# Persistent tiles of a hybrid stream encoder, put in another order in SBUF

## The chip, the cores and the metric

The kernel runs on one core of a Trainium2 chip. The metric is the device time of one execution in microseconds (us), lower is better. Three runs of the kernel before took 1451.21, 1452.49 and 1453.37 us.

## The reference, cut to what matters

One layer over 256 tokens of 2048 channels in float32. The normalised input goes through one wide projection (22672 columns) that feeds four token mixers; their outputs are projected again, gated, summed, and projected once more.

```
h = rms_norm(x, norm_g)
u = einsum('bsd,dn->bsn', h, w_in)
a_in, b_in, b_gate, c_qkv, c_f, c_gate, d_in, d_gate, m_logit = split(u)
y_a = short_conv(a_in)              # A: gated short convolution
y_b = rwkv7(b_in, b_gate, ...)      # B: RWKV-7 time mixing, 16 heads of 64
y_c = fox(c_qkv, c_f, c_gate)       # C: forgetting attention, 16 heads of 64
y_d = pooling(d_in, d_gate)         # D: causal pooling
proj = einsum('bskc,kcd->bskd', stack(y_a..y_d), w_branch)      # 4 x 1024 -> 2048
merged = sum(sigmoid(m_logit + b_merge) * proj, over the branches)
out = rms_norm(x + einsum('bsd,de->bse', merged, w_out), final_g)
```

## The kernel before, in words

Nearly all the work is matrix products of 256 tokens with weights that come from DRAM. A product is made in three single-pass matmuls: each float32 operand is split in a high part (rounded to the type F32R) and a low part (the difference), and high x high, high x low and low x high are added up in PSUM (`products`, lines 236, 237 and 238). The moving operand is a row block of weights, 128 x 512 (`wh` or `wl`); the stationary operand is a 128 x 128 piece of the transposed activations (`xh`, `xl` for the input projection; `yah`, `yal` to `ydh`, `ydl` for the branches; `mh`, `ml` for the output).

`chunk` makes 512 output columns. For each pair of row blocks (KG = 2) one DMA on SP's queue brings the raw weights (`raw`, 3 buffers), ACT writes the high parts (`wh`, 6 buffers, line 263), DVE the low parts (`wl`, 6 buffers, line 264), and TensorE runs 2 blocks of tokens x 2 row blocks x 3 matmuls. A chunk of the input projection has 16 row blocks, so 96 matmuls; one of a branch's projection has 8, so 48. In the last chunk of the output projection (`keep`) the parts of the weights lie in tiles whose contents are no longer needed: `xh`, `xl`, `ych`, `ycl`, `ydh`, `ydl`.

The program runs through branches B, C, A (in halves of 512 channels) and D; their chunks of the input projection are mixed by the scheduler with RWKV's and attention's small steps. It sets a static order by priority: weights' conversion first, then RWKV's chain, then attention's, then the rest. Then comes the merge: 4 groups of 512 columns x 4 branches, each step one chunk for the gate (96 matmuls) and one for the branch (48). The output projection is 4 chunks, and a norm and the stores end it.

Tiles are laid out in each partition in the order of the pools, and within a pool in the order in which the tiles are first asked for; each size is rounded up to 32 bytes. The pool `pers` comes first: `cst` (constants, 5120 bytes a partition), `xh`, `xl` (16384 each), then seven small tiles (`rstd`, `nrstd8`, `ngT`, `ones1`, `cq`, `fss`, `frs`: the first four where the input is read, the others further down; 352 bytes in all with rounding). Then come `wpool` (`raw`, `wh`, `wl`), `bc`, `ynat` (`yb`, `yc`, `ya`, later `mh` and the first of `ml`), `wk`, and from line 757 on `ytp` (branches' transposed outputs and `ml1`). The first byte of `pers` lies at remainder 128 modulo 512.

Of the kernel before, what the change touches and what calls it, by code (L numbers as in the profile page):

```python
# [9 lines left out]
F32 = mybir.dt.float32  # L10
F32R = mybir.dt.float32r
# [6 lines left out]
P = 128  # L18
# [35 lines left out]
    ("cmask", 384),  # L54
# [10 lines left out]
def make_constants():  # L65
    """Constants of the shapes alone: masks, cumulative sums, pooling bands."""
    i = np.arange(P)[:, None]
    t = np.arange(P)[None, :]
    c = {}
    c["ident"] = (i == t)  # L70
    c["cmat"] = ((i <= t).astype(np.float32) - (i % SUB <= SUB // 2 - 1)) * (i // SUB == t // SUB)
    c["tri"] = (i <= t)
    c["ones"] = np.ones((P, P))
    c["rmask"] = np.concatenate([(i % SUB < t[:, :SUB]), (i % SUB <= t[:, :SUB])], axis=1)
    caus = np.where(i >= t, 0.0, -NEG)
    c["cmask"] = np.concatenate([caus, np.zeros((P, P)), caus], axis=1)
    slot = np.arange(P) % 32
    rep = slot // NH
    ii = np.arange(32)[None, :, None]
    cc = np.arange(8)[None, None, :]  # L80
    c["eye32"] = (ii == rep[:, None, None] * 8 + cc).reshape(P, 256)
    consts = np.concatenate([np.asarray(c[n], np.float32).reshape(P, w) for n, w in _CONST_COLS], axis=1)
    s = np.arange(T)[:, None]
    t = np.arange(T)[None, :]
    bands = []
    for win in POOL_WINDOWS:
        band = ((s <= t) & (s > t - win)).astype(np.float32) / np.minimum(t + 1, win) - (s == t)
        bands.append(band[:P])
        bands.append(band[P:, P:])
    bands = np.concatenate(bands, axis=1).astype(np.float32)  # L90
    return np.ascontiguousarray(consts), np.ascontiguousarray(bands)
# [3 lines left out]
def kernel(  # L95
# [38 lines left out]
    # ---------------------------------------------------------------- pools  # L134
# [11 lines left out]
    # Of what is ready, the scheduler takes the weights' conversion first, then the chains of  # L146
    # small steps of branches B and C, then the rest in the order of the program.
# [10 lines left out]
    # ------------------------------------------------------------ constants  # L158
# [5 lines left out]
    def K(name):  # L164
        lo, hi = _COFF[name]
        return cst[:, lo:hi]
# [3 lines left out]
    def bcast(src, n=CH, pool=bc_pool):  # L170
        """A row of DRAM on every partition."""
        t = pool.tile([P, n], F32, name="row", bufs=2)
        gp.dma_start(out=t, in_=src.unsqueeze(0).to_broadcast([P, n]))  # L173
        return t
# [7 lines left out]
    # ----------------------------------------------------- input, RMS, x^T  # L182
    xh = pers.tile([P, D // P, T], F32R, name="xh")
    xl = pers.tile([P, D // P, T], F32R, name="xl")
    rstd = pers.tile([P, NB], F32, name="rstd")
    nrstd8 = pers.tile([P, NB], F32, name="nrstd8")
    ngT = pers.tile([P, D // P], F32, name="ngT")
    ones1 = pers.tile([P, 1], F32, name="ones1")
# [8 lines left out]
    def x_quarter(q):  # L197
        """x^T * norm_g, split in two parts, of 512 channels; the sums of squares for the norm."""
        xt = xin.tile([P, NB, CH], F32, name=f"x{q}")
        nc.sync.dma_start(out=xt, in_=x_v[:, :, q * CH:(q + 1) * CH])  # L200
        if q == 0:
            tp = psum_ex("c")
            nc.tensor.transpose(tp[:, 0:16], ng16, ident[:16, :16])
            v.tensor_copy(out=ngT, in_=tp[:, 0:16])
        for k2 in range(2):
            tp = psum_ex("c" if k2 else "r")
            for j in range(2):
                for b in range(NB):
                    c0 = (2 * k2 + j) * P
                    nc.tensor.transpose(tp[:, j * T + b * P:j * T + (b + 1) * P], xt[:, b, c0:c0 + P], ident)  # L210
            for j in range(2):
                k = q * 4 + k2 * 2 + j
                s = tp[:, j * T:(j + 1) * T]
                sc.activation(out=xh[:, k, :], in_=s, func=AF.Copy, scale=ngT[:, k:k + 1])
                v.scalar_tensor_tensor(out=xl[:, k, :], in0=s, scalar=ngT[:, k:k + 1],
                                       in1=xh[:, k, :].bitcast(F32), op0=ALU.mult, op1=ALU.subtract)
        return xt
# [13 lines left out]
    # --------------------------------------------- products in three passes  # L231
# [11 lines left out]
    def chunk(ranges, nk, sth, stl, before=lambda g: None, keep=None):  # L243
        """[T, n] = st^T @ w for column ranges (view [P, nk, .] in DRAM, first, number) of the weights.
        With keep, where the parts of all the weights have place, the second tokens follow the first."""
# [36 lines left out]
    def silu_psum(dst, ps):  # L282
        """dst = silu(rstd * ps) on [P, NB, CH]."""
# [6 lines left out]
    def gate(dst, ps):  # L290
        """dst *= silu(rstd * ps) on [P, NB, CH]."""
# [7 lines left out]
    def shift(dst, src, n):  # L299
        """dst[t] = src[t - n], zero before the first token; [P, NB, cols]."""  # L300
# [5 lines left out]
    # ------------------------------ the first chunk, with the input beside it  # L306
# [21 lines left out]
    # ---------------------------------------------------- RWKV-7 (branch B)  # L328
# [11 lines left out]
    def hbc(t):  # L340
        """[P, n] -> [P, n, H]."""
        return t.unsqueeze(2).to_broadcast([P, t.shape[1], H])

    def rwkv_prep(hf, u):
        """Everything of a half (8 heads) that is made in [token, channel]: u and what is returned."""
# [9 lines left out]
        # decay and in-context learning rate  # L355
        s = rw.tile([P, NB, HALF], F32, name="s")
        a = rw.tile([P, NB, HALF], F32, name="a")
        # three products of parts, the two with the high part of the weights in one
# [18 lines left out]
        # the norm of the keys goes to one side: kk kk^T / |kk|^2  # L377
# [9 lines left out]
        # keys scaled by the in-context learning rate  # L387
# [5 lines left out]
        # bonus weights per head  # L393
# [6 lines left out]
        # decay from the middle of one sub-block to the middle of the next  # L400
# [11 lines left out]
        # decays relative to the middle of each sub-block  # L412
        ba = rw.tile([P, NB, HALF], F32, name="pv")
        for b in range(NB):
# [11 lines left out]
            # b and k of each sub-block on the two halves of the partitions  # L426
# [4 lines left out]
        # values of even sub-blocks on the upper partitions  # L431
# [4 lines left out]
    def rwkv_block(hf, b, u, prep):  # L436
        """128 tokens, two sub-blocks, of 8 heads."""
# [4 lines left out]
        # [a | r | b | k] with channels on partitions, a pair of heads at a time  # L442
# [15 lines left out]
        # products of tokens: G[b | k of s, head, sub-block, a | r of t], with s before t  # L458
# [12 lines left out]
        # inverse of the 32x32 diagonal blocks by substitution: a quadrant holds (sub-block, block),  # L471
        # a partition of it a head and 8 of the 32 columns
# [23 lines left out]
        # 32 -> 64: the block above the diagonal is U00 M01 U11  # L496
# [18 lines left out]
        # of each sub-block: what its keys' removals turn out to be (lower half), its values (upper half)  # L515
        uv1 = rw.tile([P, HALF], F32, name="e2")
        sc.activation(out=uv1[hi], in_=vv[hi], func=AF.Copy)
        for e in range(2):
# [3 lines left out]
            # z (lower half) and y (upper half) from the state, from the keys of the sub-block  # L522
# [34 lines left out]
        # norm over each head, bonus, gate  # L557
# [23 lines left out]
    # ------------------------------------- low-rank inputs and forget gates  # L581
    cq = pers.tile([P, NB, 16], F32, name="cq")
    loraT = rw.tile([P, 2, T], F32R, name="loraT")

    def lora_and_forget(lu, cf):
# [10 lines left out]
        # the high part of each on its half of the partitions, the low part on the other  # L596
# [5 lines left out]
        # cumulative log forget gates c[t, head]  # L602
        bfb = bcast(fox_bf[0], 16)
        v.tensor_tensor(out=cf, in0=cf, in1=mid(bfb), op=ALU.add)
        fa = wk.tile([P, NB, 16], F32, name="fa")
# [13 lines left out]
    # ------------------------------------------------------- FoX (branch C)  # L619
# [19 lines left out]
    def fox_head(hf, h, qa, ka, vt):  # L639
# [13 lines left out]
        for b, s in ((0, slice(0, P)), (1, slice(P, 3 * P))):  # L653
            # the logits are negated: their least is minus the maximum
            v.tensor_tensor_reduce(out=pt[:, s], in0=lg[:, s], in1=K("cmask")[:, s], scale=1.0, scalar=-2 * NEG,  # L655
# [19 lines left out]
    # ------------------------------------------------ short conv (branch A)  # L675
# [24 lines left out]
    # ------------------------------------------------------------- schedule  # L700
    def b_inputs(hf):
        t = [rw.tile([P, NB, HALF], F32, name="u" + nm) for nm in "rkv"]
        c0 = O_B + hf * HALF
        for j in range(3):
            if j == 2 and hf == 1:
                # the last columns of v with those of the low-rank inputs and the forget gates
# [49 lines left out]
    # -------------------------------------------- transposed branch outputs  # L756
# [3 lines left out]
    def split_T(dst, k0, src, nk):  # L760
        """dst (high, low parts)[:, k0 + k, token] from src [token, block, channel]."""
# [19 lines left out]
    # --------------------------------------------------- pooling (branch D)  # L781
# [30 lines left out]
    # ------------------------------------------------------- gated merge  # L812
# [15 lines left out]
    # ------------------------------------- output projection, final norm  # L828
# [12 lines left out]
    # the last weights' parts take the place of x^T and of two branches' outputs  # L841
# [9 lines left out]
    fss = pers.tile([P, NB, 4], F32, name="fss")  # L851
    frs = pers.tile([P, NB], F32, name="frs")
# [56 lines left out]
```

## Time and profile before

| | |
|---|---|
| median of 3 runs | 1452.49 us |
| profiled execution, span from first to last instruction | 1453.2 us |
| TensorE (PE) busy | 1424.5 us, 98% |
| weight loads (PEld) | 1147.8 us, 79% |
| VectorE (DVE) | 987.4 us, 68% |
| ScalarE (ACT) | 738.1 us, 51% |
| moved by DMA | 266.24 MB, mean 183 GB/s |

The profiled execution is known by its span alone, and the span stands within the three runs. A matmul's busy time runs to the modelled end of a pipelined instruction, so neighbours overlap; how fast matmuls follow each other is read from their start times in the timeline.

### The profile page before, as it was taken

The numbers are of one execution on the slowest core, as the hardware profiler recorded it, in microseconds if no ns is written. First come the engines' busy times: TensorE is split into PE (matmuls) and PEld (weight loads), VectorE is DVE, ScalarE is ACT, GpSimd is POOL, SyncE is SP. The second block draws the span as 40 slices with busy tenths as digits, with TensorE's granted clock in tenths as the row PEclk, the third lists the DMA queues.
The fourth block names the chain that finished last, engine by engine and source line by source line (L and its number), as shares of the span: only waits on it lengthen the run. The fifth ranks groups of instructions, "written<-read, shape, count | busy, mean of one in ns | idle before, by whom it ended". The sixth has DMA issues, their size and how long they took to land.

```text
span 1453.2 us, 19581 instructions
## 1 busy us (share of the span) xinstructions
PE 1424.5 (98%) x6913; PEld 1147.8 (79%) x6913; DVE 987.4 (68%) x1719; ACT 738.1 (51%) x1278; POOL 68.5 (5%) x135
## 2 busy tenths in 40 slices
PE   7999999999999999999999999999999999999997
PEld 5887778887877678887888888888888888888886
DVE  4558888599766889579957656565666556556654
ACT  6455645654455455554435544444445444444554
POOL 2110000001011000010000000000000000000000
PEclk9999999999999999999999999999999999999999
DMA  8776545446557645545544566666666666676664
GB/s 251 198 217 200 175 131 174 131 146 196 161 174 205 185 144 176 158 143 185 189 145 145 169 194 198 198 187 202 198 187 191 198 196 193 222 226 194 196 204 146
DMA packets 136626, 266.24 MB, mean 183 GB/s; under 512 B 11577, under 2 KB 15848, under 8 KB 136528
## 3 DMA queue, kind: packets, MB, share of 16 engines
q1 hardware_dynamic: 128768, 240.95, 52.4%
q0 software_dynamic: 7760, 24.04, 6.6%
q8 instruction: 54, 0.88, 0.3%
q14 instruction: 44, 0.36, 0.1%
HBM read 257.51 MB, written 2.10 MB: 179 GB/s over the span
## 4 chain that ended last, share of the span: by engine, by line
PE 81%; DVE 7%; DMA 6%; issue 3%; ACT 2%; POOL 0%; SPq 0%; ACTq 0%; DVEq 0%; POOLq 0%
PE psm L237 24%; PE psm L238 24%; PE psm L236 24%; DVE wl L264 3%; DMA raw<-in_w_in_dram 2%; DVE MT L478 1%; PE ps_r L464 1%; DMA pv<-ur 1%; DMA cg<-pz 1%; ACT wh L263 1%; PE ps_r L537 1%; DMA pv<-uv 1%; DVE tm L485 1%; PE ps_z L554 1%; PE ps_c L804 1%
## 5 line engine op out<-in xcount | busy, mean ns | idle before, releaser
L263 ACT ACTIVATE wh<-raw 128x512 fp32r<-128x512 f32 (+1 forms) x896 | 547.4, 624 | 553.7 <-PE psm L238 386.9
L264 DVE TENSOR_TENSOR wl<-raw,wh 128x512 fp32r<-128x512 f32 (+1 forms) x896 | 599.1, 681 | 327.0 <-ACT wh L263 323.5
L237 PE MATMUL psm<-wl,xh 128*128 128x512 f32 (+1 forms) x1440 | 570.5, 397 | 4.3 <-DVE wl L264 3.7
L238 PE MATMUL psm<-wh,xl 128*128 128x512 f32 (+1 forms) x1440 | 569.6, 397 | 0.0
L236 PE MATMUL psm<-wh,xh 128*128 128x512 f32 (+1 forms) x1440 | 552.6, 396 | 4.6 <-ACT wh L263 4.3
L237 PEld LDWEIGHTS psm<-wl,xh 128*128 128x128 f32 x1440 | 271.4, 189 | 71.6 <-DVE wl L264 10.5
L236 PEld LDWEIGHTS psm<-wh,xh 128*128 128x128 f32 x1440 | 271.0, 189 | 70.2 <-ACT wh L263 7.5
L238 PEld LDWEIGHTS psm<-wh,xl 128*128 128x128 f32 x1440 | 271.7, 189 | 59.2 <-issue 1.2
L485 DVE TENSOR_TENSOR tm<-UQ,MT 128x16 f32<-128x16 f32 (+30 forms) x124 | 52.8, 426 | 2.0
L487 DVE TENSOR_REDUCE UQ<-tm 128x8 f32<-128x16 f32 (+30 forms) x124 | 36.3, 292 | 1.8
L173 POOL DMA_DIRECT2D row<-in_b_merge_dram x16 | 8.6, 539 | 516.1 <-DVE qa L740 444.3
L478 DVE STREAM_TRANSPOSE MT<-G 32x1024 f32<-32x1024 f32 x16 | 32.0, 2000 | 0.3
L740 DVE SCALAR_TENSOR_TENSOR qa<-psm,rstd,row 128x512 f32<-128x512 f32 x32 | 24.0, 751 | 10.9 <-PE psm L238 10.2
L238 PE MATMUL psm<-wh,yal 128*128 128x512 f32 x64 | 25.3, 395 | 0.0
L238 PE MATMUL psm<-wh,ybl 128*128 128x512 f32 x64 | 25.3, 395 | 0.0
L238 PE MATMUL psm<-wh,ycl 128*128 128x512 f32 x64 | 25.3, 395 | 0.0
L238 PE MATMUL psm<-wh,ydl 128*128 128x512 f32 x64 | 25.3, 395 | 0.0
L657 ACT ACTIVATE pt<-pt,mx 128x128 f32<-128x128 f32 (+1 forms) x32 | 14.4, 451 | 21.4 <-DVE mx L655 21.3
L237 PE MATMUL psm<-wl,yah 128*128 128x512 f32 x64 | 25.3, 395 | 0.0
L237 PE MATMUL psm<-wl,ybh 128*128 128x512 f32 x64 | 25.3, 395 | 0.0
L237 PE MATMUL psm<-wl,ych 128*128 128x512 f32 x64 | 25.3, 395 | 0.0
L237 PE MATMUL psm<-wl,ydh 128*128 128x512 f32 x64 | 25.3, 395 | 0.0
(378 smaller groups left out, 1369.3 us busy)
## 6 DMA issues: line engine op xcount, KB each, us to landing
raw<-in_w_in_dram SPq DMA_DIRECT2D x344, 512.0 KB, 4.1
raw<-in_w_branch_dram SPq DMA_DIRECT2D x64, 512.0 KB, 4.9
raw<-in_w_out_dram SPq DMA_DIRECT2D x32, 512.0 KB, 4.7
row<-in_b_merge_dram POOLq DMA_DIRECT2D x16, 256.0 KB, 4.3
raw<-in_w_in_dram SPq DMA_DIRECT2D x8, 328.0 KB, 4.6
raw<-in_w_in_dram SPq DMA_DIRECT2D x8, 312.0 KB, 3.8
x<-in_x_dram SPq DMA_DIRECT2D x4, 512.0 KB, 9.0
cg<-pz POOLq DMA_DIRECT2D x4, 448.0 KB, 4.3
```

Of the source, the lines that this page charges most:

```text
L236: nc.tensor.matmul(o, lhsT=sth[:, k, cols], rhs=h, start=k == 0, stop=False)
L237: nc.tensor.matmul(o, lhsT=sth[:, k, cols], rhs=l, start=False, stop=False)
L238: nc.tensor.matmul(o, lhsT=stl[:, k, cols], rhs=h, start=False, stop=k == nk - 1)
L263: sc.activation(out=h[:, :n], in_=raw[:, j, :n], func=AF.Copy)
L264: v.tensor_tensor(out=l[:, :n], in0=raw[:, j, :n], in1=h[:, :n].bitcast(F32), op=ALU.subtract)
L464: nc.tensor.matmul(gps[par][:, j * P:(j + 1) * P], lhsT=bk(rows, p, e), rhs=ar(rows, p, e), start=True, stop=True)
L478: v.transpose(out=MT[32 * q:32 * q + 32].rearrange("p t (r u) -> p t r u", u=NH), in_=src)
L485: v.tensor_tensor(out=tm[:, :, 0:n], in0=UQ[:, i:32, :].rearrange("p j c -> p c j"), in1=MT[:, i:32, i].unsqueeze(1).to_broadcast([P, 8, n ...
L487: v.tensor_reduce(out=UQ[:, i, :], in_=tm[:, :, 0:n], axis=AX.X, op=ALU.add)
L537: nc.tensor.matmul(ups[lo, hs], lhsT=UF[:, h, e, :], rhs=z[:, hs], start=True, stop=True)
L554: nc.tensor.matmul(zy[hi, hs], lhsT=G[:, h, e, SUB:P], rhs=uv[:, hs], start=ch == 0, stop=ch == 0 or h == NH - 1)
L740: v.scalar_tensor_tensor(out=gt[:, b, :], in0=ps[b], scalar=rstd[:, b:b + 1], in1=bm, op0=ALU.mult, op1=ALU.add)
```

## The change

The small tiles of `pers` are asked for first, with `fss` and `frs` among them and a new persistent `fa` (128 bytes; it was a tile of `wk`), then `xh` and `xl`, then `cst`. The attention mask `cmask` is stored with 256 columns in place of 384: the first 128 of the old three blocks repeated the last, so the two uses read other columns of the same contents. Comments and doc strings are gone, so line numbers differ by 4 (line 236 is line 240 after). The cut diff:

```diff
-    ("cmask", 384),
+    ("cmask", 256),
...
-    c["cmask"] = np.concatenate([caus, np.zeros((P, P)), caus], axis=1)
+    c["cmask"] = np.concatenate([np.zeros((P, P)), caus], axis=1)
...
-    cst = pers.tile([P, N_CONST], F32, name="cst")
...
-    xh = pers.tile([P, D // P, T], F32R, name="xh")
-    xl = pers.tile([P, D // P, T], F32R, name="xl")
     rstd = pers.tile([P, NB], F32, name="rstd")
     nrstd8 = pers.tile([P, NB], F32, name="nrstd8")
     ngT = pers.tile([P, D // P], F32, name="ngT")
     ones1 = pers.tile([P, 1], F32, name="ones1")
+    cq = pers.tile([P, NB, 16], F32, name="cq")
+    fss = pers.tile([P, NB, 4], F32, name="fss")
+    frs = pers.tile([P, NB], F32, name="frs")
+    fa = pers.tile([P, NB, 16], F32, name="fa")
+    xh = pers.tile([P, D // P, T], F32R, name="xh")
+    xl = pers.tile([P, D // P, T], F32R, name="xl")
+    cst = pers.tile([P, N_CONST], F32, name="cst")
...
-    cq = pers.tile([P, NB, 16], F32, name="cq")
...
-        fa = wk.tile([P, NB, 16], F32, name="fa")
...
-        for b, s in ((0, slice(0, P)), (1, slice(P, 3 * P))):
+        for b, s, ms in ((0, slice(0, P), slice(P, 2 * P)), (1, slice(P, 3 * P), slice(0, 2 * P))):
-            v.tensor_tensor_reduce(out=pt[:, s], in0=lg[:, s], in1=K("cmask")[:, s], scale=1.0, scalar=-2 * NEG,
+            v.tensor_tensor_reduce(out=pt[:, s], in0=lg[:, s], in1=K("cmask")[:, ms], scale=1.0, scalar=-2 * NEG,
...
-    fss = pers.tile([P, NB, 4], F32, name="fss")
-    frs = pers.tile([P, NB], F32, name="frs")
```

The order of the instructions is nearly the same on every engine; a few early ones change places. TensorE in the second chunk of branch B, before (rows of split products; `psm` is their sum in PSUM):

```order
73 L238 MATMUL psm<-wh,xl 128x512
74 L236 MATMUL psm<-wh,xh 128x512
75 L237 MATMUL psm<-wl,xh 128x512
76 L238 MATMUL psm<-wh,xl 128x512
77 L236 MATMUL psm<-wh,xh 128x512 x2
78 L237 MATMUL psm<-wl,xh 128x512
```

and in the changed kernel:

```order
73 L242 MATMUL psm<-wh,xl 128x512
74 L240 MATMUL psm<-wh,xh 128x512 x2
75 L241 MATMUL psm<-wl,xh 128x512
76 L242 MATMUL psm<-wh,xl 128x512
77 L240 MATMUL psm<-wh,xh 128x512
78 L241 MATMUL psm<-wl,xh 128x512
```

One high x high matmul has moved ahead of a pair of others; from there on TensorE's order is the same to the end. DVE behind the input's norm, before (`nrstd_80` is `nrstd8`):

```order
17 L228 RECIPROCAL rstd<-ssum 128x2
18 L229 TENSOR_SCALAR nrstd_80<-rstd 128x2
19 L264 TENSOR_TENSOR wl<-raw,wh 128x512 x2
20 L215 SCALAR_TENSOR_TENSOR xl<-ps_r,ngT,xh 128x256
21 L215 SCALAR_TENSOR_TENSOR xl<-ps_c,ngT,xh 128x256
```

and in the changed kernel:

```order
17 L232 RECIPROCAL rstd<-ssum 128x2
18 L268 TENSOR_TENSOR wl<-raw,wh 128x512
19 L233 TENSOR_SCALAR nrstd_77<-rstd 128x2
20 L268 TENSOR_TENSOR wl<-raw,wh 128x512
21 L219 SCALAR_TENSOR_TENSOR xl<-ps_r,ngT,xh 128x256
22 L219 SCALAR_TENSOR_TENSOR xl<-ps_c,ngT,xh 128x256
```

One conversion of weights stands a place earlier, before a small instruction; one other conversion, a few rows on, changes places with a piece of `xl` (on ACT with a piece of `xh`). On SP's queue the second load of constants has 1024 columns in place of 1152, at the same place.

## Rows read from the trace of the kernel before

**Rows 1.** Page: busy us (share of the span) x instructions; granted clock in tenths
```profile
PE 1424.5 (98%) x6913; PEld 1147.8 (79%) x6913; DVE 987.4 (68%) x1719; ACT 738.1 (51%) x1278; POOL 68.5 (5%) x135
...
PEclk9999999999999999999999999999999999999999
```
**Rows 2.** Waits of TensorE, whole span: us in total, times, longest us
```profile
PE ps_r L210 <- DMA x<-in_x_dram: 4.9, 1, 4.9
PE psm L236 <- ACT wh L263: 4.3, 8, 1.0
PE psm L237 <- DVE wl L264: 3.7, 7, 1.2
PE ps_c L203 <- DMA cst<-in_consts_dram: 3.1, 1, 3.1
```
**Rows 3.** Stretches: length, busy us of each engine, clock, DMA share, GB/s
```profile
0.00:813.00 813.00, 792.34 (x4176) 637.89 (x4177) 606.83 (x1144) 426.15 (x782) 56.83 (x114) 1.00 0.57 174
813.00:1353.00 540.00, 540.00 (x2335) 434.81 (x2334) 323.63 (x483) 264.35 (x411) 10.59 (x19) 1.00 0.64 198
1353.00:1446.00 93.00, 92.20 (x405) 75.11 (x403) 55.33 (x87) 45.34 (x82) 1.07 (x2) 1.00 0.55 182
```
**Rows 4.** Chain of waits, shares by line, from 0 to 813, then 505 to 813
```profile
by line: PE psm L237 17.7%; PE psm L238 17.6%; PE psm L236 17.6%; issue 5.2%; DVE wl L264 5.0%; DMA raw<-in_w_in_dram 4.0%; DVE MT L478 2.0%; PE ps_r L464 2.0%; DMA pv<-ur 1.7%; DMA cg<-pz 1.4%; ACT wh L263 1.2%; PE ps_r L537 1.1%; DMA pv<-
...
by line: PE psm L238 23.4%; PE psm L237 23.3%; PE psm L236 23.2%; DVE MT L478 2.6%; PE ps_r L464 2.4%; PE ps_c L804 2.4%; DMA raw<-in_w_in_dram 1.6%; DVE wl L264 1.5%; PE ps_z L530 1.4%; PE ps_z L554 1.4%; PE ps_r L537 1.4%; PE ps_c L798 1.
```
**Rows 5.** Timeline of TensorE, one merge step's gate: start us, us, line, tiles
```profile
1153.27 0.39 PE L236 MATMUL psm<-wh,xh 128*128 128x512 f32 x1
1153.50 0.39 PE L237 MATMUL psm<-wl,xh 128*128 128x512 f32 x1
...
1156.07 0.39 PE L236 MATMUL psm<-wh,xh 128*128 128x512 f32 x1
...
1186.87 0.39 PE L236 MATMUL psm<-wh,xh 128*128 128x512 f32 x1
```
**Rows 6.** Timeline of TensorE, branch projections: the merge's first, the same step's
```profile
837.91 0.39 PE L236 MATMUL psm<-wh,yah 128*128 128x512 f32 x1
...
1175.67 0.39 PE L236 MATMUL psm<-wh,ych 128*128 128x512 f32 x1
...
1178.47 0.39 PE L236 MATMUL psm<-wh,ych 128*128 128x512 f32 x1
```
**Rows 7.** Timeline of TensorE, output projection, first two chunks
```profile
1359.83 0.39 PE L238 MATMUL psm<-wh,ya 128*128 128x512 f32 x1
...
1361.87 0.39 PE L236 MATMUL psm<-wh,yb 128*128 128x512 f32 x1
...
1366.22 0.39 PE L236 MATMUL psm<-wh,yb 128*128 128x512 f32 x1
...
1367.58 0.39 PE L236 MATMUL psm<-wh,yc 128*128 128x512 f32 x1
...
1370.35 0.39 PE L236 MATMUL psm<-wh,yc 128*128 128x512 f32 x1
```
**Rows 8.** Timeline of TensorE, output projection, last chunk
```profile
1422.62 0.40 PE L236 MATMUL psm<-xh,yb 128*128 128x512 f32 x1
...
1428.24 0.40 PE L236 MATMUL psm<-ych,yc 128*128 128x512 f32 x1
```
**Rows 9.** Page: groups (count, busy us, mean ns, idle before); a DMA (KB, us to landing)
```profile
L263 ACT ACTIVATE wh<-raw 128x512 fp32r<-128x512 f32 (+1 forms) x896 | 547.4, 624 | 553.7 <-PE psm L238 386.9
L264 DVE TENSOR_TENSOR wl<-raw,wh 128x512 fp32r<-128x512 f32 (+1 forms) x896 | 599.1, 681 | 327.0 <-ACT wh L263 323.5
L237 PE MATMUL psm<-wl,xh 128*128 128x512 f32 (+1 forms) x1440 | 570.5, 397 | 4.3 <-DVE wl L264 3.7
L237 PEld LDWEIGHTS psm<-wl,xh 128*128 128x128 f32 x1440 | 271.4, 189 | 71.6 <-DVE wl L264 10.5
...
raw<-in_w_in_dram SPq DMA_DIRECT2D x344, 512.0 KB, 4.1
```

More of the change, by code (lines that the diff above doesn't have):

```diff
@@ L156, in level @@
         at[n], tc.cur_priority = tc.cur_priority, own
+    rstd = pers.tile([P, NB], F32, name="rstd")
+    nrstd8 = pers.tile([P, NB], F32, name="nrstd8")
+    ngT = pers.tile([P, D // P], F32, name="ngT")
+    ones1 = pers.tile([P, 1], F32, name="ones1")
+    cq = pers.tile([P, NB, 16], F32, name="cq")
[4 more added lines that the diff above has]
+    xl = pers.tile([P, D // P, T], F32R, name="xl")
     cst = pers.tile([P, N_CONST], F32, name="cst")
@@ L180, in flat @@
         return t.rearrange("p a b -> p (a b)")
-    xh = pers.tile([P, D // P, T], F32R, name="xh")
-    xl = pers.tile([P, D // P, T], F32R, name="xl")
[L185 to L188, printed above, removed]
     gp.memset(ones1, 1.0)
```

## The prediction

> **What bounds the kernel now.** I read the page's busy times first. [...] The list of waits comes next: over the whole run TensorE waits for a handful of events only, the largest 4.9 us once, 4.3 us in 8 times, 3.7 us in 7 times [rows 2]. The view by stretches then splits the span: up to 813 us (branches A to D) TensorE is busy for 792.34 us, in the gated merge (813 to 1353 us) for 540.00 of 540.00 us, in the output projection for 92.20 of 93.00 us [rows 3]. DVE has work for only 323.63 us of the merge. So the merge and the output projection go at the rate of the matmuls and of nothing else. In the first 813 us the chain of waits says how far this holds: lines L236 to L238 make 17.6 + 17.6 + 17.7 = 52.9% of it, the rest are small RWKV and attention steps, DVE, DMA and issue [rows 4].
>
> So the question is how long one 128x512 matmul takes, from its start to the next one's. A busy time of about 396 ns [rows 9] does not answer that, since the matmuls are pipelined and overlap in the record; the start times in the timeline do. The trace of before holds the comparison that the change makes, because the tiles already stand in different relations. Worked out from the tile sizes (allocation in steps of 32 bytes), the remainders modulo 512 of the start addresses are: `xh`, `xl` 128; `raw`, `wh`, `wl` 480; `ya`, `yb`, `yc` 480 (which hold the merged `mh`, `ml[0]` at the end); the `ytp` tiles (`yah` to `ydl`, `ml1`) 96. All slices of 128 tokens or 512 columns add multiples of 512. Four relations of moving and stationary operand result:
> - 480 with 128, the input projection: from 1153.27 to 1156.07 us 12 matmuls start, 2.80 / 12 = 233.3 ns each; a whole merge step of 96 + 48 matmuls goes from 1153.27 to 1186.87, 33.60 / 144 = 233.3 ns [rows 5].
> - 480 with 96, the branch projection: 1175.67 to 1178.47, again 2.80 / 12 = 233.3 ns [rows 6].
> - 480 with 480, output projection from `yb` and `ya`: 9 matmuls from 1359.83 to 1361.87, 2.04 / 9 = 226.7 ns, and 6 from 1366.22 to 1367.58, 1.36 / 6 = 226.7 ns [rows 7].
> - The very next ones, same weights' tiles and same stage, `yc` at 480 but `ml1` at 96, so that one load in three is at another remainder: 1367.58 to 1370.35, 2.77 / 12 = 230.8 ns [rows 7].
> And in the last chunk, moving 128 with stationary 480: 1422.62 to 1428.24, 5.62 / 24 = 234.2 ns [rows 8]. Within one chunk the pace changes at the matmul where the tile changes. Each matmul runs beside the weight load of the next (189 ns, [rows 9]); with equal remainders the pair is 233.3 - 226.7 = 6.6 ns cheaper. [...]
>
> [...]
>
> **The change part by part.** In the new order eight small tiles come first (32 + 32 + 64 + 32 + 128 + 32 + 32 + 128 = 480 bytes, so `xh` starts at remainder 96), then `xh`, `xl` (16384 bytes each) and `cst` (4608 bytes, 9 x 512), all multiples of 512. So `raw`, `wh`, `wl`, `ya`, `yb`, `yc` start at 96 too, and the `ytp` tiles stay at 96. Every split matmul then stands in the relation "equal".
> A. Merge: 16 steps of 144 matmuls = 2304, each 6.6 ns shorter: 15.2 us. All of it is on the path, since TensorE has no idle time there [rows 3]. What comes late next: per two rows of weights TensorE takes 12 x 0.227 = 2.72 us, ACT 2 x 0.62 = 1.25, DVE 2 x 0.68 = 1.36, and the transfer lands 4.1 us after its issue with three `raw` buffers to fill [rows 9]. Nothing of these reaches 2.72 us a step, so the cover holds.
> B. Output projection: of 3 chunks the halves with `yc`, `ml1`, 3 x 48 = 144 matmuls, from 230.8 to 226.7: 0.6 us. The last chunk's 96 from 234.2 to 226.7: 0.7 us. The other 144 are there already.
> C. First 813 us: 27 full chunks x 96 = 2592 matmuls (3 x 1440 of [rows 9], less 192 with 328 columns, less 16 x 96 of the merge), at most 2592 x 6.6 = 17.1 us. Of the chain 0.529 x 813 = 430 us are such matmuls, that is 430 / 0.2333 = 1843 of them, worth 12.2 us. The chain is one path: where TensorE gets ahead, it meets the same DMA or DVE result a little later in the queue, and waits there instead. Lower end 0 (every gain is waited away again), upper end 17.1; between them the stretch 505 to 813, 69.9% on the chain [rows 4], alone gives 0.699 x 308 / 0.2333 x 6.6 ns = 6.1 us. I take 10, nearest to the chain's row.
> D. 192 matmuls of 328 columns are not shown in an equal relation: between 0 and 192 x 6.6 ns = 1.3 us; I take 0.5. Transposes have `ident` (in `cst`) moving, which goes from 128 to 96; the trace has no such pair. By the same step on 323 of them they could gain or lose 323 x 6.6 = 2.1 us; I take 0.
> E. The rest: `cmask` is read at other columns by instructions of the same size and 64 KB less of constants are loaded behind the input; `fa` has its own tile. A few conversions change places with a small DVE or ACT instruction in the first 130 us. I cost these at nothing: TensorE's cover there is thin, so one conversion (0.68 us) either way is the bound.
>
> Sum: 15.2 + 1.3 + 10 + 0.5 = 27.0 us. 1453.2 - 27.0 = 1426.2 for an execution like the profiled one; the median of the runs, 1452.5, lies 0.7 below its span, so about 1425.5 to 1426. I forecast 1426.
>
> **The rivals.**
> 1. The first 813 us give nothing back (C and D 0): TensorE's gain turns into waits for `wl`, `wh` or a shifted copy. For it: the waits of rows 2 all lie there, and 47% of that chain isn't a split matmul. Against: 52.9% is. Time 1452.5 - 16.5 = 1436.
> 2. The whole of C and D is gained: 1452.5 - 16.5 - 18.4 = 1417.6.
> 3. No effect: the quick matmuls are quick because of the tiles or their place, not the relation of addresses. For it: only 480 with 480 is seen; 96 with 96 is not seen in a run of split matmuls. Against: `wh` at the same address is slow or quick by its partner, and the sign is the same for two different partners. Time 1452.5.
> 4. Slower: remainder 96 on both sides is the bad case, the two read streams hit the same place at once, and 480 with 480 is spared for another reason. Price: one more step of 6.6 ns above 233.3, on the same 2304 + 240 matmuls of A and B and the 1843 of C: 4387 x 6.6 = 29 us, 1481. It decides as soon as the pace in the merge is above 233.3 ns; the rows speak against it, since no relation measured there is over 234.2.
>
> **How the numbers follow.** Forecast case (relation holds, C partly gained, 1420 to 1432): 0.72. Rival 1 and what lies near it (1432 to 1438): 0.12. Rival 2: 0.05. Rival 3: 0.07. Rival 4: 0.04. The range from 1419 to 1438 holds the forecast, rival 1 and a part of rival 2, some 0.86. Faster by over 0.2% (2.9 us, about what a measurement can tell from no change): 0.72 + 0.12 + 0.05 = 0.89; the same 0.07; slower 0.04.
>
> **What would show it.** Step A: in the merge 12 matmuls start in 2.72 us and a step of 144 takes 32.6 to 32.7 us; 33.6 would mean rival 3, over 33.6 rival 4. Step B: `yc` and `ml1` at the pace of `yb` and `ya`, and the last chunk too. Step C: the first merge matmul on `yah` starts about 10 us before its 837.91 us of now [rows 6]; the waits of TensorE for `wl` and `wh` grow from 8.0 us to some 12. If the pace in the merge is 226.7 and the time still over 1438, C was wrong in sign; if the merge keeps its pace, the reading of the timeline was.

## The result and the profile after

The changed kernel takes 1432.83 us (median of 4 runs, 1430.55 to 1436.84); the kernel before, run beside it, 1452.77 us (1451.21 to 1453.37). The ratio is 0.9859 (95% interval 0.9845 to 0.9873), 1.4% faster. The forecast was 1426, the range 1419 to 1438: the time lies inside, 7 us above the forecast. The profiled execution spans 1431.5 us and took 1433.31, so 1.8 us lie around a span. By that the profiled execution of before, 1453.2 us long, took some 1455.0, longer than all four runs beside it and 2.2 us longer than their median; its span alone, set beside their times, hid this. From span to span the change is worth 21.7 us, from median to median 19.9.

Where it came from is read stage by stage. The page and the view by stretches of the changed kernel (length, busy us and instructions of PE, PEld, DVE, ACT, POOL, granted clock, DMA share, GB/s), against [rows 1, 3]:

```profile
PE 1398.8 (98%) x6913; PEld 1146.2 (80%) x6913; DVE 984.4 (69%) x1719; ACT 736.0 (51%) x1278; POOL 68.5 (5%) x135
```
```profile
0.00:808.00 808.00, 784.10 (x4186) 638.25 (x4187) 606.17 (x1146) 425.55 (x784) 56.80 (x114) 0.99 0.60 175
808.00:1334.00 526.00, 526.00 (x2338) 435.54 (x2337) 323.04 (x485) 264.11 (x411) 10.59 (x19) 1.00 0.68 204
1334.00:1425.00 91.00, 88.71 (x393) 72.43 (x391) 53.57 (x86) 44.80 (x81) 1.08 (x2) 1.00 0.55 180
```

The merge is still TensorE from end to end, 526.0 us in place of 541.1 (1355.73 - 814.63 before): 15.1 us. The first part, up to the first gate chunk, ends 6.7 us earlier (807.96 against 814.63); behind the merge nothing remains of the 1.3 us that were forecast. DVE's and ACT's busy times differ by 0.3% from those of before. The first matmul of the merge, before and after:

```profile
814.63 0.40 PE L236 MATMUL psm<-wh,xh 128*128 128x512 f32 x1
...
807.96 0.39 PE L240 MATMUL psm<-wh,xh 128*128 128x512 f32 x1
```

The timeline of TensorE shows the pace, in the same merge step as [rows 5, 6]:

```profile
1137.21 0.39 PE L240 MATMUL psm<-wh,xh 128*128 128x512 f32 x1
...
1139.93 0.39 PE L240 MATMUL psm<-wh,xh 128*128 128x512 f32 x1
...
1158.97 0.39 PE L240 MATMUL psm<-wh,ych 128*128 128x512 f32 x1
...
1161.69 0.39 PE L240 MATMUL psm<-wh,ych 128*128 128x512 f32 x1
...
1169.85 0.39 PE L240 MATMUL psm<-wh,xh 128*128 128x512 f32 x1
```

12 matmuls in 2.72 us, on `xh` and on `ych` alike, and 144 in 32.64: 226.7 ns each, where it was 233.3. In the output projection the tiles that were slow in [rows 7] now run like their neighbours, 2.72 us for 12 in place of 2.77:

```profile
1345.82 0.39 PE L240 MATMUL psm<-wh,yc 128*128 128x512 f32 x1
...
1348.54 0.39 PE L240 MATMUL psm<-wh,yc 128*128 128x512 f32 x1
```

The chain of waits of the first part (0 to 803 us) looks different. Split matmuls make 32.6% of it, against 52.9% in [rows 4]; DVE's conversions and transfers have taken their place:

```profile
by line: PE psm L241 10.9%; PE psm L242 10.9%; PE psm L240 10.8%; DVE wl L268 10.1%; issue 7.6%; DMA raw<-in_w_in_dram 7.5%; DVE tm L489 3.6%; DMA cg<-pz 2.5%; DVE UQ L491 2.3%; DVE MT L482 2.0%; DMA pv<-ur 1.8%; ACT wh L267 1.7%; PE ps_r L
```

And the waits of TensorE (us in total, times, longest), against [rows 2]:

```profile
PE psm L241 <- DVE wl L268: 6.6, 13, 1.0
...
PE psm L240 <- ACT wh L267: 3.4, 7, 1.0
...
PE psm L240 <- ACT ydh L267: 0.7, 1, 0.7
```

Waits for `wl` went from 7 to 13 times, those for `wl` and `wh` together from 8.0 to 10.0 us. The last line is new and lies in the last chunk of the output projection.

### The profile page after: what moved, and what is told of

Read it like the earlier page. It is cut to its first block, busy times and chain, and to the rows that moved or that the text cites. A ratio compares the mean times of both kernels' runs of the same rounds, so it can differ in the third digit from the quotient of the medians.

```text
span 1431.5 us, 19581 instructions
## 1 busy us (share of the span) xinstructions
PE 1398.8 (98%) x6913; PEld 1146.2 (80%) x6913; DVE 984.4 (69%) x1719; ACT 736.0 (51%) x1278; POOL 68.5 (5%) x135
## 4 chain that ended last, share of the span: by engine, by line
PE 67%; DVE 15%; DMA 11%; issue 4%; ACT 2%; POOL 1%; SPq 0%; ACTq 0%; DVEq 0%; POOLq 0%
PE psm L242 20%; PE psm L241 20%; PE psm L240 20%; DVE wl L268 6%; DMA raw<-in_w_in_dram 4%; DVE tm L489 2%; DMA cg<-pz 1%; DVE UQ L491 1%; DVE MT L482 1%; DMA raw<-in_w_out_dram 1%; DMA pv<-ur 1%; ACT wh L267 1%; PE ps_r L468 1%; PE ps_r L541 1%; DMA pv<-uv 1%
## 5 line engine op out<-in xcount | busy, mean ns | idle before, releaser
L241 PE MATMUL psm<-wl,xh 128*128 128x512 f32 (+1 forms) x1440 | 563.8, 393 | 7.0 <-DVE wl L268 6.6
L242 PE MATMUL psm<-wh,xl 128*128 128x512 f32 (+1 forms) x1440 | 562.1, 392 | 0.0
```

The costliest lines, as they stand in the source:

```text
L241: nc.tensor.matmul(o, lhsT=sth[:, k, cols], rhs=l, start=False, stop=False)
L242: nc.tensor.matmul(o, lhsT=stl[:, k, cols], rhs=h, start=False, stop=k == nk - 1)
```

## The experiments

**Apart again.** Is it the relation of the addresses, or something else in the change? The changed kernel with a pad behind `cst`, which moves everything behind it:

```diff
     cst = pers.tile([P, N_CONST], F32, name="cst")
+    pad = pers.tile([P, 96], F32, name="pad")
+    gp.memset(pad[:, 0:1], 0.0)
```

> The changed kernel with a 384-byte pad behind `cst`: the weights' tiles go from remainder 96 to 480, so input-projection matmuls (4128) stand 480 with 96 again, while branch and most output matmuls stay equal (480 with 480). Order, `cmask`, `fa` as in the changed kernel. Theory (equal remainders are what helps): gate chunks of the merge back at 233.3 ns a matmul, branch chunks at 226.7; a merge step of 144 takes 96 x 0.2333 + 48 x 0.2267 = 33.28 us against 32.6; the time is 1447 to 1450 us. Rival (the gain comes from the order, `cmask`, `fa` or from remainder 96 as a place): 1433 us and 32.6 us a step, or, if only the place 96 helps, branch chunks slow too and 1452 us.

Measured: 1446.78 us (1444.95 to 1448.62), 0.9946 of before (0.9932 to 0.9960). The same merge step in its timeline (line 242 is the first of the three products):

```profile
1113.45 0.41 PE L242 MATMUL psm<-wh,xh 128*128 128x512 f32 x1
...
1135.77 0.40 PE L242 MATMUL psm<-wh,ybh 128*128 128x512 f32 x1
...
1146.69 0.40 PE L242 MATMUL psm<-wh,xh 128*128 128x512 f32 x1
```

96 gate matmuls (480 with 96) in 22.32 us, 232.5 ns; 48 branch matmuls (480 with 480) in 10.92 us, 227.5 ns; the step 33.24 us, forecast 33.28. The median came out just under the expected 1447 to 1450. Order, `cmask` and `fa` are those of the changed kernel, so they are not what made the gate chunks quick: with the addresses apart these are slow again, while the branch chunks, whose addresses agree, stay quick. In the first part this profile is 3 us ahead of that of before (the first matmul on `yah` starts at 834.96 us, against 837.91), 1.7 of them by one stretch at half the granted clock less (see below).

**Together, without the new order.** The kernel before, with `cmask` at 256 columns as in the change, and a pad that brings the weights to the remainder of `xh` (the pad's part of the diff):

```diff
     frs = pers.tile([P, NB], F32, name="frs")
+    pad = pers.tile([P, 40], F32, name="pad")
+    gp.memset(pad[:, 0:1], 0.0)
```

> The kernel before, its tiles' order kept, with `cmask` at 256 columns (for room) and a 160-byte pad at the end of the persistent tiles: weights' tiles and `xh`, `xl` all at remainder 128; the branches' transposed tiles at 256, so branch matmuls stay unequal. Theory: gate chunks at 226.7 ns, branch chunks at 233.3, a merge step 96 x 0.2267 + 48 x 0.2333 = 32.96 us; against before 10.1 us in the merge and 6 to 7 in the first part: 1435 to 1437 us. Rival (only the changed order or remainder 96 helps): 1452 us.

Measured: 1438.18 us (1436.90 to 1438.80), 0.9886 of before (0.9870 to 0.9903).

```profile
1106.01 0.39 PE L236 MATMUL psm<-wh,xh 128*128 128x512 f32 x1
...
1127.78 0.40 PE L236 MATMUL psm<-wh,ybh 128*128 128x512 f32 x1
...
1138.93 0.39 PE L236 MATMUL psm<-wh,xh 128*128 128x512 f32 x1
```

The mirror image: gate 21.77 / 96 = 226.8 ns (128 with 128), branch 11.15 / 48 = 232.3 ns (128 with 256), the step 32.92 us, forecast 32.96. The time is 15.6 us under the 1453.77 of before on that chip, where 16 to 17 were forecast, and 1.2 us above the expected 1435 to 1437.

**Which distances?** Two kernels, each with its six weight buffers at six distances from `xh`, by pads between them (`PADS` holds the steps; the lines for the list and for a last pad are left out here):

```diff
-                        h = wpool.tile([P, CH], F32R, name="wh", bufs=6)
-                        l = wpool.tile([P, CH], F32R, name="wl", bufs=6)
+                        i = turn[0] % 6
+                        first = turn[0] < 6
+                        turn[0] += 1
+                        if first and PADS[i]:
+                            wpool.tile([P, PADS[i] // 4], F32, name=f"pad{i}")
+                        h = wpool.tile([P, CH], F32R, name=f"wh{i}", bufs=1)
+                        l = wpool.tile([P, CH], F32R, name=f"wl{i}", bufs=1)
```

> The changed kernel with each of the six buffers of `wh`, `wl` at its own remainder: distance of moving from stationary operand 0, 32, 64, 128, 256, 384 bytes modulo 512, every sixth row block each. Theory (only distance 0 is quick): from one start to the next 226.7 ns at 0 and 233.3 ns at the other five. Rival (the memory repeats at a shorter step): 256 or also 128 as quick as 0. Second rival: some distance is quicker than 0, under 226 ns.

> As the run before with distances 96, 160, 192, 224, 320, 352 bytes. Theory: 233.3 ns at all six, no buffer at 226.7; time near 1450 us. Rivals: one of them at 226.7 or below; or one clearly above 233.3.

Measured: 1449.14 and 1451.85 us, one run each, against 1453.77 for the kernel before on that chip. The table has the mean distance of starts in ns, over the matmuls behind 800 us with `wh` or `wl` moving that stand between two others at the same distance (122 to 164 starts each, those under 260 ns, worked out from the start times in the trace and the order of the buffers):

| moving minus stationary, modulo 512 | 0 | 32 | 64 | 96 | 128 | 160 | 192 | 224 | 256 | 320 | 352 | 384 |
|---|---|---|---|---|---|---|---|---|---|---|---|---|
| ns | 232.6 | 232.3 | 232.0 | 234.3 | 233.9 | 232.1 | 231.5 | 231.1 | 234.4 | 231.3 | 234.8 | 231.7 |

All twelve lie between 231.1 and 234.8, none is under 226, and 0 is in their midst: one in nine of its starts is at 227 and below, three quarters are at 233 and above. So the expected 226.7 for every sixth row block did not come: among buffers at other distances a row block at distance 0 is not quick. In the last chunk of the output projection of the same run, where moving and stationary operands are all equal, the mean is 228.3 ns (88 starts). Here the gain came in a run of equal pairs only, and these two runs therefore can't say which distances would be quick in a run of their own.

Runs of one distance stand in the other traces. Over the matmuls behind 800 us with the five before and the six behind at the same distance (starts under 260 ns apart), the mean is 226.8 ns at distance 0 (2598 starts, changed kernel), 233.1 at 128 (22 starts, last chunk of the kernel with the pad behind `cst`), 234.1 at 160 (22 starts, last chunk of the kernel before), 233.4 at 352 (1390 starts, its input projection) and 233.4 at 384 (592 starts, its branch projections; 232.3 and 232.4 in the two kernels with pads above). So 0 is the only quick one of five. The other distances are not tested in runs, 256 among them.

**Another place.** The same pad of 384 bytes ahead of `xh`, so that all operands are equal at remainder 480.

> The changed kernel with a 384-byte pad ahead of `xh`: all operands of the split matmuls are equal as before, but at remainder 480 in place of 96. Theory (only the relation counts): 226.7 ns a matmul, 32.6 to 32.7 us a merge step, the same time as the changed kernel within 0.3%. Rival (the place counts too): the pace differs from 226.7 by more than 1 ns and the time by 5 us or more.

Measured: 1433.27 us (1432.41 to 1433.97), 0.9853 of before (0.9837 to 0.9868).

```profile
1137.73 0.39 PE L242 MATMUL psm<-wh,xh 128*128 128x512 f32 x1
...
1139.77 0.39 PE L242 MATMUL psm<-wh,xh 128*128 128x512 f32 x1
...
1170.37 0.39 PE L242 MATMUL psm<-wh,xh 128*128 128x512 f32 x1
```

9 matmuls in 2.04 us and a step of 32.64 us: as at 96, and as the gate chunks at 128 in the run with the pad. At these three remainders the place does not count. The changed kernel itself took 1432.54 us on this chip (below).

**Where the rest of the first part's gain went.** Two pairs, each with the layout of before and of after, and a part of DVE's work left out. The first has no low parts of the weights (`wl` is left out, `wh` is used twice):

```diff
-                        l = wpool.tile([P, CH], F32R, name="wl", bufs=6)
+                        l = h
...
-                    v.tensor_tensor(out=l[:, :n], in0=raw[:, j, :n], in1=h[:, :n].bitcast(F32), op=ALU.subtract)
                     wh.append(h)
-                    wl.append(l)
+                    wl.append(h)
...
-                products(ps, sth, stl, *keep(k), k, nk, n, 1)
+                products(ps, sth, stl, keep(k)[0], keep(k)[0], k, nk, n, 1)
```

> The kernel before without the low parts of the weights: DVE's conversion (line 264) is left out and the high part is used in its place, so DVE loses some 600 us of work, TensorE has the same matmuls at the same addresses. It is one of a pair with the next run; by itself it should be faster than before by the waits that go through DVE's conversions in the first 813 us: some 5 to 25 us, 1428 to 1448 us.

> The changed kernel with the same part left out (no low parts of the weights). Theory: in the changed kernel the first part gained only 6 to 7 of some 14 us because DVE's conversions wait in DVE's queue behind RWKV's small steps. Then the gap between this pair is larger than 20 us: 15 in the merge, 1 behind it, 10 to 13 in the first part, so 26 to 29 us, and the merge starts 10 to 13 us earlier than in its partner. Rival (transfers and the issue of DMAs take the gain): the first part still gains 6 to 7, the gap is 22.

Measured: 1430.52 (1429.86 to 1431.38) and 1406.29 us (1404.47 to 1410.08), a gap of 24.2, between the theory's 26 to 29 and the rival's 22. The first gate chunk starts at 790.81 and 786.05 us: in these profiles the first part gains 4.8 us, not 10 to 13. But the profiled execution of the second, 1410.08 us, is the slowest of its four, and it spent three short stretches at half the granted clock where its partner had none. By the table below these cost 5.1 us, so without them it would be 9.9. Neither the theory nor the rival is shown.

The second pair leaves out 30 of the 31 steps of the substitution that inverts RWKV's diagonal blocks (`for i in range(30, 29, -1)` in place of `range(30, -1, -1)`):

> The kernel before with one step in place of 31 of the substitution that inverts RWKV's diagonal blocks (left out: 240 small DVE instructions). One of a pair with the next run. Faster than before by what of that chain is on the path: 0 to 20 us.

> The changed kernel with the same steps of the substitution left out. Theory (DVE's queue in the RWKV stretches takes the gain): the first part gains 8 to 11 us against its partner, and the gap of the pair is 24 to 27 us. Rival (it is not this chain, but conversions that wait for transfers): the first part gains 6 to 7 and the gap is 20 to 22.

Measured: 1454.01 (1450.03 to 1455.12) and 1427.99 us (1426.31 to 1429.00), a gap of 26.0, which agrees with the theory's number. The first gate chunk starts at 813.56 and 801.54, 12.0 us apart. But here too the granted clock has a part: two half-clock stretches in the first profile, none in the second.

**The changed kernel once more.**

> The changed kernel once more, on one chip with the next two. Theory on the first part: a wait of TensorE is followed, in some executions, by 3.4 us at half the granted clock, which costs 1.7 us each; the trace of before had two such stretches in its first 813 us, that of the changed kernel three. If so, the executions spread by such steps (spans of 1428 to 1435 us, higher where the mean clock is lower), and in this profile the start of the merge moves against the 814.6 us of before by 6.6 us with three stretches, by 8 to 10 with two or one. Rival: the first part gains 6.6 us whatever the clock does.

Measured: 1432.54 us (1431.78 to 1436.10), 0.9853 of before (0.9835 to 0.9870). In this profile the first gate chunk starts at 810.37 us, so the first part gained 4.3 us only, and with two stretches at half the clock, not three. The expectation failed: the clock is a term, but not the whole. Nor do the spans follow the mean clock: the longest of the four, 1434.3 us, had 0.996, the shortest, 1430.0, had 0.994. The trace of the changed kernel shows what such a stretch is, in its timeline (idle time before an instruction in brackets) and the view by stretches (the eighth number is the granted clock):

```profile
582.55 1.19 PE L507 MATMUL ps_r<-X,G 32*32 32x32 f32 x32
584.73 0.33 PE L664 MATMUL ps_c<-cst,pt 128*128 128x128 f32 x1 [0.98 <-ACT pt L659]
...
586.25 0.63 PE L240 MATMUL psm<-wh,xh 128*128 128x512 f32 x1
586.68 0.63 PE L241 MATMUL psm<-wl,xh 128*128 128x512 f32 x1
```
```profile
575.00:585.70 10.70, 9.72 (x74) 8.01 (x73) 10.48 (x22) 6.52 (x13) 0.00 (x0) 1.00 0.58 165
585.90:589.10 3.20, 3.20 (x11) 2.42 (x9) 1.48 (x3) 1.26 (x2) 0.00 (x0) 0.50 0.76 245
```

TensorE works on 32x32 pieces, waits 0.98 us for attention's exponentials, and shortly after the granted clock stands at 0.50: matmuls start 0.43 us apart, each some 0.2 us late, 1.6 us in all (1.7 by the stretch's length, 3.4 us, and half the clock).

The first part of each profile, worked out from the start times (us; "ordinary" are distances of split matmuls under 245 ns, what each is over 227; "long" those above, what each is over 227, with a few other matmuls of 512 columns among them; half-clock stretches from the trace's clock records; "new waits" is the growth of "long" less 1.7 for each more stretch):

| pair or run | first part earlier by | ordinary, before and after | long, before and after | stretches, before and after | new waits |
|---|---|---|---|---|---|
| changed kernel | 6.7 | 15.1, 3.9 | 40.9, 47.4 | 2, 3 | 4.8 |
| once more | 4.3 | 15.1, 4.0 | 40.9, 49.1 | 2, 2 | 8.2 |
| another place | 6.1 | 15.1, 3.8 | 40.9, 44.7 | 2, 3 | 2.1 |
| no low parts | 4.8 | 15.4, 2.9 | 25.6, 33.0 | 0, 3 | 2.3 |
| no substitution | 12.0 | 15.3, 3.5 | 40.4, 40.3 | 2, 0 | 3.3 |

In every pair the ordinary matmuls give 11 to 12.5 us, and 2 to 8 us go to new waits, whichever part of DVE's work is missing. The 12.0 of the pair without the substitution owes 3.4 us to two half-clock stretches that happened not to occur. With the stretches taken off at 1.7 us each, the first part is earlier by 8.4, 4.3, 7.8, 9.9 and 8.6 us, in the table's order: the pairs with less work on DVE lie at the upper end of what the changed kernel shows by itself, not clearly beyond it. The ratios to before say much the same: 0.9993 less 0.9828 and 0.9844 less 0.9680 are 24 us each, with intervals of some 3 us, the changed kernel's 20 to 21 with 2 to 3. Neither pair shows which engine takes the gain.

**A try to give it back.** The short convolution's products and sums on GpSimd, to free DVE's queue (`gp.tensor_tensor` for `v.tensor_tensor` in three lines of `conv_half`, ten operations):

> The changed kernel with the short convolution's products and sums (five 128x1024 operations in each half, 1.13 us each on DVE) on GpSimd. If DVE's queue is what holds back conversions in these stretches, the waits for `wl` shrink and the first part ends 1 to 4 us earlier: 1429 to 1432 us. Rival: GpSimd is slower and the shifted copies are issued from its queue, behind these operations; the convolution's chain grows and the time is 1433 to 1440 us.

Measured: 1448.24 us (1445.04 to 1450.06), 0.9953 of before (0.9937 to 0.9970), some 16 us slower than the changed kernel's 1432.54 beside it. One of GpSimd's groups (count, busy us, mean ns, idle before), and the stretch of the first convolution:

```profile
L694 POOL TENSOR_TENSOR cg<-cg,row 128x1024 f32<-128x1024 f32 x4 | 10.4, 2589 | 14.6 <-DMA cg<-pz 14.6
```
```profile
345.00:380.00 35.00, 30.94 (x169) 23.85 (x169) 28.56 (x52) 10.21 (x20) 6.79 (x7) 0.76 0.50 146
```

An operation takes 2.6 us in place of the 1.2 us on DVE (1221 ns in the changed kernel's trace, not the 1.13 us of the expectation), with 14.6 us of waits for the shifted copies over both halves; TensorE's waits for `wl` grew to 12.1 us in place of shrinking. In the stretch shown TensorE stands idle for 4 of 35 us and runs at a mean clock of 0.76, which costs it some 8 us more (an estimate: 0.24 x 35). Here a later chain cost twice, in the wait and in the clock. The rival held in its sign; its price, up to 1440 us, was 8 us short.

## Why the prediction was right, and where its sizes were off

- The reading of the timeline was right: 233.3 ns where the remainders differ, 226.7 where they agree, in runs of such matmuls. The two pad runs undo and do that one thing (the gate chunks go from 226.7 to 232.5 ns with the one, from 233.3 to 226.8 with the other), the place run takes away rival 4 (the bad remainder), and rival 3 (no effect) is gone with the merge step at 32.64 us. Why equal remainders are quicker is not shown; the weight loads take 189 ns in the traces of before and after alike.
- The time, 1432.83, lies in the range, but just beyond the 1420 to 1432 of the forecast case, in the stretch that had been given 0.12. Of the 7 us over the forecast, 3.8 lie in steps C and D, 1.4 in B, 0.1 in A, the rest in the base.
- Step A, 15.2 us: measured 15.1. No cover failed, TensorE is busy 526.00 of 526.00 us.
- Step B, 1.3 us: the first three chunks take 66.2 in place of 66.9 us, 0.7 gained as worked out, but from the last chunk's start to the end it took 0.8 more (31.3 against 30.5). The chunk's first half comes with its weights: the chain holds a transfer of 5.06 us from 1403.92 on, then the conversion into `ydh`, and TensorE waits 0.70 us at 1409.69. I had weighed this cover for the merge alone. In the other runs this last piece takes 30.0 to 31.7 us with either layout, so 0.8 is within its spread.
- Step C, 10 us: the step that was mis-sized, 6.7 in the profile and 4.3 in the next one, with the 328-column matmuls of step D in it (33.16 to 31.72 us of starts, waits and all; those under 170 ns apart went from 151.4 to 149.5 ns, 0.4 us for all 192, where 0.5 was taken). The signs named for it went the way that was named, but less far: the first merge matmul on `yah` starts 7.2 us earlier, not 10, and the waits for `wl` and `wh` grew to 10.0 us, not 12. Three parts: the estimate of 2592 matmuls at 6.6 ns counts those too that wait anyway or stand beside other work (ordinary distances held 15.1 us over 227 ns, and 3.9 of that stayed); of what the ordinary ones gave (11.2 us) 2 to 8 us came back as waits; and half-clock stretches came and went, 1.7 us each. I multiplied the chain's share, 430 us, by the saving and took off a fifth for other chains. The chain of after shows how much else was close behind: split matmuls make 32.6% of it in place of 52.9.
- The clock: the sum has no term for it, and the page shows a 9 in every slice [rows 1]. A 9 is 90% or more, and two stretches of the first part of before stand at half, 1.7 us each. One of them (length, busy us of each engine, clock, DMA share, GB/s):

```profile
154.40:157.60 3.20, 3.20 (x9) 2.53 (x8) 3.20 (x6) 1.26 (x2) 0.00 (x0) 0.50 0.44 136
```

- The base: I set a span, 1453.2 us, beside run times, which are 1.8 us longer than their spans. So the profiled execution was 2.2 us slower than the median, not 0.7. From span to span the change gave 21.7 us of the 27.0 forecast, from median to median 19.9.
- What the waits of the first part hang on stays open. DVE's conversions are the ones named with the most time (6.6 and 9.2 us in two profiles), but the pair without them gained 24.2 us in all, where the changed kernel gained 20 to 22, and its profiles do not settle where.

## What to carry to other kernels

Read the pace of matmuls from their start times, stage by stage, and where it differs at the same shape and clock, compare the operands' addresses: one stage that is quick by luck shows what the others could be. Size the small persistent tiles so that the big operands of split matmuls agree modulo 512 bytes (here 226.7 ns a matmul in place of 233.3). Where a pad of 160 bytes made them agree, it gave the same pace as the new order (226.8 ns), but in runs of equal pairs: among pairs at other distances, those at 0 averaged 232.6 ns. Price such a gain in full only where TensorE has no idle time (15.1 of 15.2 us came in the merge); where chains ran beside it, some half of what the chain's share said was left here (6.7 and 4.3 of 12.2 us). Look at what the granted clock does after each new wait (here it stood at 0.50 for 3.4 us shortly after one of 0.98 us).

## What the runs showed that I had not expected

- A matmul's pace went with its neighbours': pairs at distance 0 among buffers at other distances averaged 232.6 ns, as slow as those others, in a run of equal pairs 226.7 to 227.5.
- Of the five distances seen in runs, 0 alone was quick: 226.8 ns, against 232.3 to 234.1 at the other four.
- Stretches at half the clock stand in the first part of 10 of the 13 profiles, each within 3 us of a wait of TensorE of 0.5 to 2.6 us. Nine profiles have one at 152 to 155 us; the others are spread (38, 453 to 458 and 586 us more than once). Many waits have none behind them; what decides is not shown.
